# A hybrid decoder step on one core: cross-half scores one step later, and three sets of 128x128 tiles turned by VectorE in 32x32 blocks instead of by TensorE

## The chip, the cores and the metric

One core of one Trainium2 chip runs the whole step. The metric is the device time in microseconds (us) of the launch, as the median of several runs. The engines are named as the profile names them: PE (TensorE, matmuls; PEld its weight loads), DVE (VectorE), ACT (ScalarE), POOL (GpSimd), SP (SyncE). Engines run their own instruction queues and wait for each other by semaphores; a DMA is issued by an instruction in one engine's queue and lands later.

## The reference, cut to what matters

One decoder layer, 256 prompt tokens and 8 sample tokens (264 columns), model width 2048:

```python
z = h @ w_in                                   # 2048 -> one wide projection for three mixers
y_a = spatial_gating(u, layernorm(v), w_s, b_s)    # A: s = (w_s * lower triangle) @ v per 128-token chunk and group, 8 groups
o_hg, S_hg = gated_linear_recurrence(q, k, v, log_f, s0)   # B: HGRN2, 8 heads
o_g, S_g = gated_linear_recurrence(...)                     # C: GLA, 4 heads
merged = sum over n of gates[n] * (branches[n] @ w_branch[n])
x = x + gt1 * rmsnorm(merged @ w_out)
y2 = square(relu(h2 @ w_mlp_up)) @ w_mlp_down   # 2048 -> 8192 -> 2048
x = x + gt2 * rmsnorm(y2)                       # wanted with tokens in rows
```

Recurrence per head and token: `S = diag(f) S + k v^T`, `o = S^T q`, with `f` from `log_f`. `w_s` has the shape 8 x 128 x 128. Outputs are the two y, the recurrences' last states, and the normalised v rows.

## The kernel before, in words

**Layout and the weight stream.** Activations stand channels in partitions, tokens along the row ("turned", 264 columns). Each product with a weight matrix is done as three fp32r matmuls per 128x128 weight tile (whi with xh, whi with xl, wlo with xh). A *granule* is 512 KB of weights, 4 k-tiles by 2 output tiles, so 24 matmuls of 128x264 into one PSUM tile `mm` (`granule`, L713). `Stream` (L635) loads the raw weights on SP's queue into 4 buffers, casts them to `whi` on ACT (L673) and subtracts to get `wlo` on DVE (L677), two 128x512 halves per granule, into 6 split buffers; the splits run two granules ahead of the matmuls.

**What sets the order.** The program is written out granule by granule. After each granule `background()` (L785) advances a step counter `now`, runs what stands in the list `later`, and pumps three queues of generators: `bt` for turned rows, `bg` for the mixers, `bs` for the samples' recurrences. A generator that yields `READY` is not resumed before the next step. `slot()` (L747) places collected small products (the mixers' 32x32 level products, the samples' products, the ada products) between granules. In the first part, up to the projection, every engine keeps the program's order; in the mixers PE and POOL do, and in the last phase (the MLP) only PE, the other engines' order being set by the tile scheduler.

**Turning by `Rows`.** `Rows` (L837) turns blocks of channels x tokens: two DVE stream transposes (L850) that turn each 32x32 square in place, a DMA of 512 KB to DRAM scratch `rows_d` (L853), and one step or more later four DMAs of 128 KB back (L859), which put the squares where they belong. Both kinds of DMA are issued by POOL. `gone()` does the transposes and the DMA out; the rows come back by way of `bt`.

**Mixer A** (`mixer_a`, L948). `wsT`, the eight turned tiles of `w_s` times the triangle `triu`, is made by eight PE transposes in two groups of four (an identity as the weights, `cst`, into a PSUM tile `sm`) and two DVE multiplications out of PSUM (L139). `w_s` is the third of four constants that come by `const_a` at granules 8, 10, 12 and 14 of the last chunk but one, after `cst` and the masks at granule 7.

**Mixers B and C** (`mixer_r`, L1322), called for two HGRN2 groups of four heads (groups 0 and 1) and one GLA group (group 2). Within 32 tokens the scores come from level products, between 32-token blocks and 64-token blocks from cross products; last the cross-half scores: `kd` and `qd` (128 tokens to 128 tokens) are made by a subtraction, two exponentials (ACT, L1414) and two DVE multiplications (L139), `kd` is also turned by a `Rows`, and then four products of `kd` and `qd`, L1428, go to `sm` and are copied to `attx` (ACT, L1430). The output products follow, `outputs()` (L1488) turns them and copies the rows (L1497), `finish` (L1504) adds the samples' columns (PE transposes, copies L1513), and `parts_b` (L1580) multiplies by the gate (L1584) and splits the result for the branch's product with `w_branch`.

**The last down-projection** (`down`, L1857, f = NFB-1). For each output pair m = 0..6 (two granules each): the sum comes out of PSUM (L142), `gated` (L1626) scales it to `g` (128 x 2 x 264), and one step later four PE transposes (L96, `to_tokens`) put `g` with tokens in rows into PSUM, from where ACT (L1660) and DVE (L1661) copy 128x256 each into `yt`. The tail (m = 7, row sums, the last norm, the sum with x and the stores) uses `yt`.

Of the kernel before, what the change touches and what calls it, by code (L numbers as in the profile page):

```python
# [7 lines left out]
F32 = mybir.dt.float32  # L8
# [7 lines left out]
P = 128  # L16
# [19 lines left out]
CHUNKS = (2, 2, 4, 4, 4)  # L36
# [36 lines left out]
def hybrid_step_kernel(  # L73
# [55 lines left out]
    def sm(shape=None):  # L129
        return psm.tile(shape or [P, 512], F32, tag="sm", name=nm("sm"))  # L130
# [700 lines left out]
        return linear(win, 0, KT, c0, width, hH, hL)  # L831


    rows_d = dp.tile([13, P, 1024], F32, tag="rows_d", name="rows_d")
    n_turned = [0]

    class Rows:  # L837
# [67 lines left out]
    def const_a(src):  # L905
        consts_a.append(blk([P, 8, P]))
        nc.sync.dma_start(consts_a[-1], src)

    srcs_a = [
        sgu_ln_g[0].partition_broadcast(P).rearrange("p (g n) -> p g n", g=8),  # L910
        sgu_ln_b[0].partition_broadcast(P).rearrange("p (g n) -> p g n", g=8),
        sgu_w_s[0].rearrange("g n m -> n g m"),
        sgu_b_s[0].rearrange("g n -> (g n)").partition_broadcast(P).rearrange("p (g n) -> p g n", g=8),
    ]
    def to_tokens(vt):
# [30 lines left out]


    def mixer_a():  # L948
        lng, lnb, wsr, bsb = consts_a
        lng, lnb = (v.rearrange("p g n -> p (g n)") for v in (lng, lnb))  # L950
        vr, vtk = rows_a.rows, []
        wsT = blk([P, 8, P])
        w00 = tmp([P, 8], "w00", 1)
        for gg in range(2):
            ps = sm()
            for i in range(4):
                T.transpose(ps[:, i * P:(i + 1) * P], wsr[:, 4 * gg + i, :], ident)
            yield
            mul(wsT[:, 4 * gg:4 * gg + 4, :], ps.rearrange("p (g n) -> p g n", g=4), triu.unsqueeze(1).to_broadcast([P, 4, P]))
        yield  # L960
        vs = tmp([P, 8, NS], "vsa", 1)
        w8 = tmp([P, 8, NS], "vsb", 1)
        r8 = tmp([P, NS], "vsr", 1)
# [139 lines left out]
    for ci, n in enumerate(CHUNKS):  # L1103
        final = ci == len(CHUNKS) - 1
        gn = 4 // n
        ng = len(begin) // gn
        if not final:
            nxt = parts[ci].paced()
        for gi in range(ng):
            if ci or gi:  # L1110
                accs = [new_acc() for _ in range(gn)]
            todo = begin[gi * gn:gi * gn + gn]

            def evict(acc):

                c0, dst, fn = todo.pop(0)
                z = acc[:, :, 0:NT]
                if ci:
                    add(dst, dst, z)
                elif todo:  # L1120
                    S.copy(dst, z)
                else:
                    V.tensor_copy(dst, z)
                if final and fn is not None:
                    after.append((dst, fn))

            def between():

                step[0] += 1
                if not final:  # L1130
                    next(nxt, None)

            load_due()
            if ci or gi:
                granule(win, 0, n, begin[gi * gn][0], gn * CW, accs, hH, hL, k0, True, True, evict, between)
            else:
                first_granule(accs, evict, between)
            if ci == 0 and gi < 2:
                x_transposed(4 + 2 * gi, early[gi])
            if ci == 0 and 1 <= gi < 5:  # L1140
                x_transposed(2 * gi + 6)
            while after:
                dst, fn = after.pop(0)
                S.activation(dst, dst, fn)
            if final:
                if gi in (6, 12, 18):
                    rounds.steps()
                if gi in (0, 2, 6, 8, 12, 14, 18):
                    rounds.load()
                if gi in (6, 7, 8, 9):  # L1150
                    rows_a.half((gi - 6) // 2, gi % 2)
                if gi in (8, 10):
                    rows_a.out(gi // 2 - 4)
                if gi in (11, 13):
                    rows_a.back((gi - 11) // 2)
                now[0] += 1
                if gi >= 12:
                    bg.pump(1.0)
            if ci == len(CHUNKS) - 2 and 7 <= gi < 16:
                if gi == 7:  # L1160
                    nc.sync.dma_start(cst[:, 256:904], consts[:, 256:904])
                    nc.sync.dma_start(msk, masks.rearrange("p (l t) -> p l t", l=6))
                elif gi % 2 == 0:
                    const_a(srcs_a.pop(0))
        if not final:
            run(nxt)
        k0 += n
# [154 lines left out]
    def mixer_r(G):  # L1322
# [99 lines left out]
        kd_rows = Rows([kd])  # L1422
        yield from kd_rows.gone()
        yield READY
        attx = blk([P, 4, P])
        ps = sm([P, 4, P])
        for h in range(4):
# [235 lines left out]
    def block_rows(m, g):  # L1663
# [5 lines left out]
        for t in range(2):  # L1669
            squares(m, t, g, pt)  # L1670

    def norms(meanwhile):

        ps = sm([P, 2 + NS])
# [182 lines left out]
    def down(f, ah, al):  # L1857
        for m in range(8):
# [7 lines left out]
                add(dst, dst, z)  # L1866
            if f == NFB - 1:
                g = gated(m, dst, G2)
                later.append((now[0], lambda m=m, g=g: put_rows(m, to_tokens(g), yt)))

    zs = begin_up()
    order.__exit__(None, None, None)
# [3 lines left out]
    for f in range(NFB):  # L1876
        nxt = up(f + 1) if f + 1 < NFB else None
        if f == NFB - 1:
            rounds.drain()
            mul(G2, mod[:, 5 * KT:6 * KT, :], gpost2T.unsqueeze(2).to_broadcast([P, KT, NC]))  # L1880
            yt = [[blk([P, 1024]) for _ in range(2)] for _ in range(2)]
        last = pend
        down(f, *pend)
        pend = nxt
# [150 lines left out]
```

## Time and profile before

| what | value |
|---|---|
| median of 3 runs | 1780.88 us (1779.7 to 1781.59) |
| profiled execution | 1784.03 us, span 1782.2 us |
| PE busy | 1759.0 us (99%), 16866 matmuls |
| DVE busy | 1191.7 us (67%), 2094 instructions |
| ACT busy | 998.4 us (56%) |
| POOL busy | 175.6 us (10%), 293 instructions |
| bytes moved by DMA | 455.67 MB, mean 256 GB/s |

The span is the profiled execution from its first to its last instruction; the profiled execution's own time is 1.83 us longer, and 3.15 us longer than the median of the runs. Rows of the timeline give the start, the time from the first start to the last end, the engine, the line, the operation, and how many were joined (x4); in brackets stands the idle time before and what ended it. Matmuls overlap in a pipeline: one of 0.28 us follows the other at 0.11 us.

### The profile page before, as it was taken

The numbers are of one execution on the slowest core, as the hardware profiler recorded it, in microseconds if no ns is written. First come the engines' busy times: TensorE is split into PE (matmuls) and PEld (weight loads), VectorE is DVE, ScalarE is ACT, GpSimd is POOL, SyncE is SP. The second block draws the span as 40 slices with busy tenths as digits, with TensorE's granted clock in tenths as the row PEclk, the third lists the DMA queues.
The fourth block names the chain that finished last, engine by engine and source line by source line (L and its number), as shares of the span: only waits on it lengthen the run. The fifth ranks groups of instructions, "written<-read, shape, count | busy, mean of one in ns | idle before, by whom it ended". The sixth has DMA issues, their size and how long they took to land.

```text
span 1782.2 us, 42021 instructions
## 1 busy us (share of the span) xinstructions
PE 1759.0 (99%) x16866; PEld 1677.1 (94%) x16866; DVE 1191.7 (67%) x2094; ACT 998.4 (56%) x1810; POOL 175.6 (10%) x293
## 2 busy tenths in 40 slices
PE   7999999999999999999999999999999999999998
PEld 5899999999998989999999989999999999999997
DVE  5666669887786886656556666545666666666666
ACT  5444456766766666445445666555454545454554
POOL 4222010122121123200000010000000000000000
PEclk9999999999999999999999999999999999999999
DMA  9998799899999899988876847786666666666663
GB/s 352 399 346 301 240 315 302 261 327 314 323 289 298 289 327 297 374 241 271 272 249 215 306 128 239 234 265 189 197 194 196 196 197 194 198 194 197 194 195 114
DMA packets 334547, 455.67 MB, mean 256 GB/s; under 512 B 15986, under 2 KB 277984, under 8 KB 334352
## 3 DMA queue, kind: packets, MB, share of 16 engines
q1 hardware_dynamic: 312160, 381.05, 66.1%
q0 software_dynamic: 21552, 71.48, 11.6%
q8 instruction: 132, 2.16, 0.5%
q14 instruction: 63, 0.52, 0.1%
q10 hardware_dynamic: 640, 0.47, 0.1%
HBM read 434.42 MB, written 18.51 MB: 254 GB/s over the span
## 4 chain that ended last, share of the span: by engine, by line
PE 94%; DMA 2%; DVE 1%; issue 1%; ACT 1%; POOL 0%; SPq 0%; ACTq 0%; DVEq 0%; POOLq 0%
PE mm L92 85%; PE ada L92 5%; PE sm L92 3%; PE sm L96 1%; DMA raw<-in_w_in_dram 1%; DMA vbc<-vs_d 1%; DMA b<-in_x_prompt_dram 0%; DVE wlo L677 0%; DMA b<-in_w_ada_dram 0%; DVE b L142 0%; DVE b L1775 0%; DMA out_dram<-st 0%; DVE st L1306 0%; ACT b L148 0%; DVE b L145 0%
## 5 line engine op out<-in xcount | busy, mean ns | idle before, releaser
L92 PE MATMUL mm<-b,whi 128*128 128x264 f32 x9248 | 1579.0, 277 | 1.9 <-ACT gt L1549 0.9
L92 PEld LDWEIGHTS mm<-b,whi 128*128 128x128 f32 x9248 | 1395.2, 189 | 35.8 <-issue 18.2
L92 PE MATMUL mm<-b,wlo 128*128 128x264 f32 x4624 | 1276.1, 276 | 0.4 <-DVE wlo L677 0.4
L677 DVE TENSOR_TENSOR wlo<-raw,whi 128x512 fp32r<-128x512 f32 x1118 | 758.5, 689 | 427.2 <-ACT whi L673 423.3
L673 ACT CAST whi<-raw 128x512 fp32r<-128x512 f32 x1118 | 680.8, 617 | 632.0 <-DVE wlo L677 325.8
L92 PEld LDWEIGHTS mm<-b,wlo 128*128 128x128 f32 x4624 | 873.9, 189 | 0.9 <-DVE wlo L677 0.8
L142 DVE TENSOR_TENSOR b<-b,mm 128x528 f32<-128x528 f32 (+1 forms) x137 | 95.6, 699 | 72.2 <-PE mm L92 65.8
L1965 POOL TENSOR_TENSOR gs<-b,G 128x16 f32<-128x16 f32 x1 | 0.2, 221 | 714.0 <-DVE b L142 714.0
L92 PE MATMUL ada<-b,cT 128*32 128x256 f32 (+2 forms) x896 | 66.0, 425 | 1.6 <-DMA b<-in_w_ada_dram 1.4
L92 PEld LDWEIGHTS ada<-b,cT 128*32 128x32 f32 x896 | 26.6, 113 | 31.6 <-issue 17.9
L537 POOL DMA_DIRECT2D b<-in_w_ada_dram x64 | 46.3, 726 | 44.9 <-PE ada L92 35.3
L1307 POOL DMA_DIRECT2D out_dram<-st x32 | 23.5, 735 | 209.2 <-DVE st L1306 204.0
L673 ACT CAST whi<-araw 128x512 fp32r<-128x512 f32 x38 | 23.2, 619 | 27.7 <-PE mm L92 24.0
L1306 DVE SCALAR_TENSOR_TENSOR st<-vbc,b,st 128x128 f32<-128x128 f32 (+1 forms) x96 | 32.3, 390 | 6.0 <-ACT st L1304 3.2
L1304 ACT ACTIVATE st<-st,fs 128x128 f32<-128x128 f32 (+1 forms) x96 | 35.1, 427 | 1.9 <-DMA st<-in_state_gla_dram 1.9
L139 DVE TENSOR_TENSOR b<-b,b 128x512 f32<-128x512 f32 (+1 forms) x49 | 34.6, 720 | 2.0 <-ACT b L1414 0.5
L92 PE MATMUL ada<-araw,cT 128*32 128x512 f32 x256 | 34.6, 600 | 0.0
L859 POOL DMA_DIRECT2D b<-rows_d x52 | 28.6, 556 | 27.9 <-ACT whi L673 7.3
L677 DVE TENSOR_TENSOR wlo<-araw,whi 128x512 fp32r<-128x512 f32 x38 | 24.5, 685 | 1.3 <-ACT whi L673 1.3
L92 PE MATMUL sm<-b,b 128*32 128x32 f32 (+2 forms) x320 | 22.9, 237 | 2.4 <-DVE b L139 2.4
L145 DVE TENSOR_TENSOR b<-gt,b 128x528 fp32r<-128x528 f32 x32 | 22.7, 709 | 3.2
L145 DVE TENSOR_TENSOR b<-b 128x1024 f32<-128x1024 f32 (+1 forms) x24 | 24.5, 1021 | 0.1
(308 smaller groups left out, 826.5 us busy)
## 6 DMA issues: line engine op xcount, KB each, us to landing
raw<-in_w_in_dram SPq DMA_DIRECT2D x225, 512.0 KB, 5.7
raw<-in_w_mlp_down_dram SPq DMA_DIRECT2D x128, 512.0 KB, 3.6
raw<-in_w_mlp_up_dram SPq DMA_DIRECT2D x125, 512.0 KB, 3.9
araw<-in_w_ada_dram SPq DMA_DIRECT2D x64, 512.0 KB, 6.2
b<-in_w_ada_dram SPq DMA_DIRECT2D x64, 512.0 KB, 6.5
b<-in_w_ada_dram POOLq DMA_DIRECT2D x48, 512.0 KB, 9.8
raw<-in_w_branch_dram SPq DMA_DIRECT2D x48, 512.0 KB, 5.5
raw<-in_w_out_dram SPq DMA_DIRECT2D x32, 512.0 KB, 4.6
```

The costliest lines, as they stand in the source:

```text
L92: return nc.tensor.matmul(out, w, x, **kw)
L96: return nc.tensor.transpose(*a)
L139: V.tensor_tensor(o, a, b, op=ALU.mult)
L142: V.tensor_tensor(o, a, b, op=ALU.add)
L145: V.tensor_tensor(o, a, b, op=ALU.subtract)
L537: queue.dma_start(w[:, i], w1[k * P:(k + 1) * P, :, self.k0 * P:(self.k0 + self.n) * P])
L673: self.last = [S.copy(hi, raw).ins, None]
L677: self.last[1] = V.tensor_tensor(lo, raw, hi.bitcast(F32), op=ALU.subtract).ins
L859: nc.gpsimd.dma_start(t[32 * q:32 * q + 32, :].rearrange("p (s c) -> p s c", s=4), rows_d[self.d0 + i].rearrange("(s p) (q c) -> q p s c", ...
L1304: S.activation(st[:, i, :], st[:, i, :], AF.Copy, scale=fs[:, h0 + i, b:b + 1])
L1306: V.scalar_tensor_tensor(st[:, i, :], v[:, i, :], k[:, h0 + i, NP + b:NP + b + 1], st[:, i, :], ALU.mult, ALU.add)
L1307: nc.gpsimd.dma_start(G.s_out(b, h0, nh), st)
```

## The change

Three parts.

1. `mixer_r`: one more `yield READY` before the cross-half scores, in each of the three groups.
2. `w_s` is loaded first of the four constants (granule 7, ahead of `cst`; the masks move to granule 8, the other three to 10, 12 and 14). It is turned by a `Rows`: two DVE transposes at granules 11 and 13, out at 14, back at 18. `mixer_a` multiplies the landed rows by the triangle; its eight PE transposes go, and it has one yield fewer.
3. The last down-projection, m = 0..3: a new class `Pairs` collects two `g` (eight DVE transposes of 128x256 in all, L1696, two for each m), sends each pair out as 512 KB, brings it back in four DMAs one step later, and two steps after that copies it into `yt` with one ACT and one DVE copy of 128x512 (L1713). The sixteen PE transposes of these four m and their eight copies out of PSUM go. m = 4..6 stay as they were.

In the changed kernel lines up to L955 stand where they were or one off; later lines are 10 or 11 lower down (L1306 is L1316, L1584 is L1595, L1661 is L1672). `rows_d` has 16 slots instead of 13.

```diff
 def mixer_a():
-        lng, lnb, wsr, bsb = consts_a
+        _, lng, lnb, bsb = consts_a
...
         for gg in range(2):
-            ps = sm()
-            for i in range(4):
-                T.transpose(ps[:, i * P:(i + 1) * P], wsr[:, 4 * gg + i, :], ident)
+            mul(
+                wsT[:, 4 * gg:4 * gg + 4, :].rearrange("p k (s f) -> p k s f", s=4),
+                rows_w.rows[0][:, gg],
+                triu.rearrange("p (s f) -> p s f", s=4).unsqueeze(1).to_broadcast([P, 4, 4, 32]),
+            )
             yield
-            mul(wsT[:, 4 * gg:4 * gg + 4, :], ps.rearrange("p (g n) -> p g n", g=4), triu.unsqueeze(1).to_broadcast([P, 4, P]))
-        yield
...
             if ci == len(CHUNKS) - 2 and 7 <= gi < 16:
                 if gi == 7:
+                    const_a(srcs_a.pop(0))
+                    rows_w = Rows(consts_a[0:1], lambda b, r: b[:, 4 * r:4 * r + 4, :].rearrange("p k (q f) -> p k q f", q=4))
                     nc.sync.dma_start(cst[:, 256:904], consts[:, 256:904])
+                elif gi == 8:
                     nc.sync.dma_start(msk, masks.rearrange("p (l t) -> p l t", l=6))
-                elif gi % 2 == 0:
+                elif gi < 15 and gi % 2 == 0:
                     const_a(srcs_a.pop(0))
+            if ci == len(CHUNKS) - 2:
+                if gi in (11, 13):
+                    rows_w.half(0, (gi - 11) // 2)
+                if gi == 14:
+                    rows_w.out(0)
+                if gi == 18:
+                    rows_w.back(0)
...
 def mixer_r(G):
         kd_rows = Rows([kd])
         yield from kd_rows.gone()
+        yield READY
         yield READY
...
+    class Pairs:
+        def __init__(self, rows, landed, then):
+            self.rows, self.landed, self.then = rows, landed, then
+        def put(self, m, g):
+            i = m % 2
+            if i == 0:
+                self.r = Rows([None])
+                self.r.ts[0] = blk([P, 1024])
+            to = self.r.ts[0].rearrange("p (q r k f) -> p r k q f", q=4, r=2, k=4)
+            for t in range(2):
+                V.transpose(to[:, t, 2 * i:2 * i + 2], g[:, :, t * P:(t + 1) * P].rearrange("p k (q f) -> p k q f", q=4))
+            if i:
+                self.r.out(0)
+                self.soon(1, self.back, m // 2, self.r)
+        def soon(self, n, f, *a):
+            later.append((now[0] + n, lambda: f(*a)))
+            later.sort(key=lambda x: x[0])
+        def back(self, b, r):
+            r.back(0)
+            self.soon(self.landed, self.natural, b, r.rows.pop())
+        def natural(self, b, v):
+            w = slice(b % 2 * 512, b % 2 * 512 + 512)
+            for t in range(2):
+                (V.tensor_copy if t else S.copy)(self.rows[t][b // 2][:, w].rearrange("p (k s f) -> p k s f", k=4, s=4), v[:, t])
+            self.then(b, w)
...
 down, f == NFB - 1:
-                later.append((now[0], lambda m=m, g=g: put_rows(m, to_tokens(g), yt)))
+                later.append((now[0], lambda m=m, g=g: put_rows(m, to_tokens(g), yt) if m > 3 else pairs.put(m, g)))
...
+            pairs = Pairs(yt, 2, lambda b, w: None)
```

**What stands where, first place: the cross-half scores of group 1.** In these rows `b<-b,b` on DVE is an operand being made (`b_7930` is `qd`, `b_7929` is `kd`), `wlo` the splits of coming granules, `sm<-b,b 128x128 x4` on PE the four scores, `sm<-b,att` the output products behind them. PE before:

```order
L92 MATMUL mm_8050<-b_5668,wlo_7917 128x264
L92 MATMUL sm_8086<-b_7930,b_7929 128x128 x4
L92 MATMUL sm_8096<-b_4791,att 128x128 x4
L92 MATMUL mm_8050<-b_5672,whi_7963 128x264
L92 MATMUL mm_8050<-b_5673,whi_7963 128x264
L92 MATMUL mm_8050<-b_5672,wlo_7964 128x264
```

DVE before:

```order
L677 TENSOR_TENSOR wlo_7964<-raw_7818,whi_7963 128x512
L139 TENSOR_TENSOR b_7929<-b_7929,b_6628 128x1024
L677 TENSOR_TENSOR wlo_7968<-raw_7818,whi_7967 128x512
L1306 SCALAR_TENSOR_TENSOR st_7724<-vbc_7877,b_6628,st_7724 128x128 x4
L677 TENSOR_TENSOR wlo_8011<-raw_7873,whi_8010 128x512
L677 TENSOR_TENSOR wlo_8015<-raw_7873,whi_8014 128x512
L1306 SCALAR_TENSOR_TENSOR st_7875<-vbc_7937,b_6628,st_7875 128x128 x4
L142 TENSOR_TENSOR os_1207_7208<-os_1207_7208,sm_8030 128x128
L139 TENSOR_TENSOR b_7930<-b_7930,b_176 128x512
L850 STREAM_TRANSPOSE b_7974<-b_7929 128x4x4x32 x2
```

PE now, where `b_8117` is `qd` and `b_8116` is `kd`:

```order
L92 MATMUL mm_8127<-b_2727,wlo_8157 128x264
L92 MATMUL sm_8284<-b_8117,b_8116 128x128 x4
L92 MATMUL sm_8294<-b_4790,att 128x128 x4
L92 MATMUL mm_8324<-b_334,whi_8190 128x264
L92 MATMUL mm_8324<-b_335,whi_8190 128x264
L92 MATMUL mm_8324<-b_334,wlo_8191 128x264
```

DVE now:

```order
L139 TENSOR_TENSOR b_8117<-b_8117,b_176 128x512
L139 TENSOR_TENSOR b_8116<-b_8116,b_6666 128x1024
L677 TENSOR_TENSOR wlo_8100<-raw_7959,whi_8099 128x512
L677 TENSOR_TENSOR wlo_8104<-raw_7959,whi_8103 128x512
L1567 SCALAR_TENSOR_TENSOR b_7834<-gt_8038,mm_8040 128x528
L850 STREAM_TRANSPOSE b_8163<-b_8116 128x4x4x32 x2
L677 TENSOR_TENSOR wlo_8153<-raw_8005,whi_8152 128x512
L677 TENSOR_TENSOR wlo_8157<-raw_8005,whi_8156 128x512
L677 TENSOR_TENSOR wlo_8191<-raw_8073,whi_8190 128x512
```

Before, the product that makes `qd` stands on DVE behind `wlo_8011` and `wlo_8015`, which belong to the granule after the one (`whi_7963`) that PE begins right behind the scores. Now it stands ahead of `wlo_8153` and `wlo_8157`, which belong to the granule that PE ends right ahead of the scores.

**Second place: the output rows of group 1 and the start of branch 1.** On DVE, `L1497` (now `L1508`) is the copy of the landed rows, `L1513` (`L1524`) are the copies of `finish`, `L1584` (`L1595`) the gate of `parts_b`, `b<-cst,b` and the products with `cst` the start of group 2. DVE before, two pieces of one stretch:

```order
L677 TENSOR_TENSOR wlo_8525<-raw_8396,whi_8524 128x512
L1497 COPY b_8612<-b_8530 128x4x128
L1346 SCALAR_TENSOR_TENSOR b_3947<-cst,b_3947 128x264
L139 TENSOR_TENSOR b_8655<-b_3946,cst 128x1024
L1573 SCALAR_TENSOR_TENSOR b_8155<-b_8155,mm_8363 128x528
L677 TENSOR_TENSOR wlo_8564<-raw_8443,whi_8563 128x512
```

```order
L677 TENSOR_TENSOR wlo_8888<-raw_8733,whi_8887 128x512
L1513 COPY b_6750<-sm_8903 128x4x8
L1513 COPY b_8612<-sm_8907 128x4x8
L1584 SCALAR_TENSOR_TENSOR b_6750<-b_6750,vec,b_8155 128x1056
L677 TENSOR_TENSOR wlo_8892<-raw_8733,whi_8891 128x512
```

DVE now:

```order
L677 TENSOR_TENSOR wlo_8786<-raw_8674,whi_8785 128x512
L1508 COPY b_8791<-b_8716 128x4x128
L139 TENSOR_TENSOR b_8834<-b_3951,cst 128x1024
L677 TENSOR_TENSOR wlo_8819<-raw_8714,whi_8818 128x512
L1524 COPY b_6741<-sm_8840 128x4x8
L1524 COPY b_8791<-sm_8844 128x4x8
L677 TENSOR_TENSOR wlo_8823<-raw_8714,whi_8822 128x512
L1584 SCALAR_TENSOR_TENSOR b_8126<-b_8126,mm_8681 128x528
L1595 SCALAR_TENSOR_TENSOR b_6741<-b_6741,vec,b_8125 128x1056
```

Between the copy of the rows and the copies of `finish` stood 30 rows of DVE; now there are two.

**Third place: the last down-projection.** On PE, `sm<-cst,gt` are the four transposes of one m. PE before, between two granules:

```order
L92 MATMUL mm_23798<-b_22720,whi_23709 128x264
L92 MATMUL mm_23798<-b_22719,wlo_23710 128x264
L96 MATMUL sm_23833<-cst,gt_23792 128x128 x4
L92 MATMUL mm_23798<-b_23007,whi_23746 128x264
L92 MATMUL mm_23798<-b_23008,whi_23746 128x264
```

PE now, at the same two granules:

```order
L92 MATMUL mm_23804<-b_22726,whi_23715 128x264
L92 MATMUL mm_23804<-b_22725,wlo_23716 128x264
L92 MATMUL mm_23804<-b_23013,whi_23752 128x264
L92 MATMUL mm_23804<-b_23014,whi_23752 128x264
L92 MATMUL mm_23804<-b_23013,wlo_23753 128x264
```

DVE before, from one `g` to the next:

```order
L1635 TENSOR_SCALAR gt_23961<-b_15026,G_15024 128x256
L142 TENSOR_TENSOR a_2227_13612<-a_2227_13612,vt_23960 128x264
L139 TENSOR_TENSOR gs_13613<-b_15026,G_15024 128x16
L142 TENSOR_TENSOR a_2227_13612<-a_2227_13612,vt_23960 128x264
L677 TENSOR_TENSOR wlo_23994<-raw_23872,whi_23993 128x512
L677 TENSOR_TENSOR wlo_23998<-raw_23872,whi_23997 128x512
L1661 COPY b_23719<-sm_24003 128x256
L677 TENSOR_TENSOR wlo_24035<-raw_23916,whi_24034 128x512
L142 TENSOR_TENSOR b_15026<-b_15026,mm_23968 128x528
```

DVE now, where the first landed pair (`b_24001`) is copied:

```order
L1646 TENSOR_SCALAR gt_24045<-b_15032,G_15030 128x256
L142 TENSOR_TENSOR a_2232_13618<-a_2232_13618,vt_24044 128x264
L139 TENSOR_TENSOR gs_13619<-b_15032,G_15030 128x16
L1696 STREAM_TRANSPOSE b_24006<-gt_24045 128x2x4x32
L142 TENSOR_TENSOR a_2232_13618<-a_2232_13618,vt_24044 128x264
L677 TENSOR_TENSOR wlo_24078<-raw_23955,whi_24077 128x512
L1696 STREAM_TRANSPOSE b_24006<-gt_24045 128x2x4x32
L677 TENSOR_TENSOR wlo_24082<-raw_23955,whi_24081 128x512
L1713 COPY b_23725<-b_24001 128x512
L677 TENSOR_TENSOR wlo_24112<-raw_23999,whi_24111 128x512
```

PE goes from granule to granule without the transposes, DVE has two transposes for each m in place of one copy out of PSUM, and the copy of a landed pair stands ahead of `wlo_24112`.

More of the change, by code (lines that the diff above doesn't have):

```diff
@@ L831, in zin @@
         return linear(win, 0, KT, c0, width, hH, hL)
-    rows_d = dp.tile([13, P, 1024], F32, tag="rows_d", name="rows_d")
+    rows_d = dp.tile([16, P, 1024], F32, tag="rows_d", name="rows_d")
     n_turned = [0]
@@ L909, in hybrid_step_kernel @@
     srcs_a = [
+        sgu_w_s[0].rearrange("g n m -> n g m"),
         sgu_ln_g[0].partition_broadcast(P).rearrange("p (g n) -> p g n", g=8),
         sgu_ln_b[0].partition_broadcast(P).rearrange("p (g n) -> p g n", g=8),
-        sgu_w_s[0].rearrange("g n m -> n g m"),
         sgu_b_s[0].rearrange("g n -> (g n)").partition_broadcast(P).rearrange("p (g n) -> p g n", g=8),
```

## The prediction

> **What bounds the kernel now.** I read the page's busy shares first, then busy time by stage, PE's waits, and the timeline round the one long wait.
>
> ```profile
> span 1782.2 us, 42021 instructions
> PE 1759.0 (99%) x16866; PEld 1677.1 (94%) x16866; DVE 1191.7 (67%) x2094; ACT 998.4 (56%) x1810; POOL 175.6 (10%) x293
> PE 94%; DMA 2%; DVE 1%; issue 1%; ACT 1%; POOL 0%; SPq 0%; ACTq 0%; DVEq 0%; POOLq 0%
> ```
>
> PE is busy for 1759.0 of 1782.2 us and carries 94% of the chain that ended last. A term therefore counts only if it is PE work, a PE wait, or a lower granted clock. By stage (span, then busy time of PE, PEld, DVE, ACT and POOL, granted clock, DMA share, GB/s):
>
> ```profile
> 260.00:300.00 40.00, 40.00 (x355) 38.35 (x352) 34.56 (x90) 20.01 (x33) 4.03 (x7) 1.00 0.98 327
> 300.00:540.00 240.00, 240.00 (x2863) 224.45 (x2862) 193.43 (x363) 171.78 (x342) 50.69 (x82) 1.00 0.94 300
> 540.00:760.00 220.00, 216.33 (x2228) 199.61 (x2228) 158.58 (x307) 139.68 (x292) 49.40 (x79) 0.99 0.95 316
> 1730.00:1766.00 36.00, 35.87 (x320) 35.67 (x319) 27.76 (x60) 21.00 (x42) 0.00 (x0) 1.00 0.39 118
> ```
>
> The spatial weights are turned in the first row, the scores belong to the next two, the last down-projection to the last. PE has no gap in the first two; 3.67 us are missing in the third. PE's waits that fall there; one is long:
>
> ```profile
> PE sm L92 <- DVE b L139: 2.4, 1, 2.4
> ...
> PE mm L92 <- ACT gt L1549: 0.9, 1, 0.9
> ```
>
> ```profile
> 549.26 0.63 ACT L1414 ACTIVATE b<-b 128x512 f32<-128x512 f32 x1
> 549.92 0.69 DVE L139 TENSOR_TENSOR b<-b,b 128x512 f32<-128x512 f32 x1 [0.50 <-ACT b L1414]
> 550.53 1.30 DVE L850 STREAM_TRANSPOSE b<-b 128x512 f32<-128x512 f32 x2
> 550.76 1.13 PE L92 MATMUL sm<-b,b 128*128 128x128 f32 x8 [2.37 <-DVE b L139]
> ```
>
> ```profile
> 551.00:552.00 1.00, 1.00 (x10) 1.00 (x10) 1.00 (x3) 0.07 (x1) 0.00 (x0) 0.91 1.09 381
> 552.00:553.00 1.00, 1.00 (x7) 1.00 (x6) 1.00 (x2) 0.51 (x1) 0.88 (x2) 0.50 1.01 407
> 553.00:554.00 1.00, 1.00 (x7) 1.00 (x6) 0.00 (x1) 0.42 (x1) 0.43 (x1) 0.50 1.00 406
> 554.00:555.00 1.00, 1.00 (x6) 1.00 (x6) 0.00 (x0) 0.94 (x5) 0.00 (x0) 0.50 0.99 294
> 555.00:556.00 1.00, 1.00 (x10) 1.00 (x9) 0.00 (x0) 0.33 (x2) 0.00 (x0) 0.88 0.99 319
> ```
>
> These are the cross-half scores of group 1. ACT's exponential ends at 549.89, DVE's product (qd) at 550.6, and PE stood idle 2.37 us for it. Right behind the gap the granted clock falls: 0.91, 0.50 three times, 0.88. What is missing from full speed adds up to 0.09 + 1.50 + 0.12 = 1.71 us. The stall cost 2.37 + 1.71 = 4.08 us.
>
> **Part 1, the extra step: −4.08 us.** By the order of the changed program a whole granule of PE work stands between the place of the scores before and now. A granule lasts 24 matmuls, half of the 5.40 us that 48 take (rows below), 2.70 us. PE, free at 548.4, would have other work until 551.1; qd is done at 550.6. DVE also no longer has two splits of a later granule ahead of qd. So the wait goes, with 0.5 us to spare, and with it the low clock. Bounds: 0 if the operand comes as much later as PE does, −4.08 if all goes; I take all, because the group's other operand chain is unchanged in length. Groups 0 and 2 have no such wait, so the step gives nothing there. What is late next is ACT's copy to `attx` and the output products, which have a level of slack: their only reader is the same generator, one step later too. The queues passed are POOL's (kd's DMA out and back, still put out before the scores) and DVE's.
>
> [...]
>
> The whole mixer part is dealt out anew by the step and by what part 2 takes from PE: the places where PE leaves the granules' stream number 109 in the old order and 112 in the new, and six of the old ones go, so nine are new. Each such place costs PE a restart, priced next.
>
> **Parts 2 and 3, PE's transposes: −0.88 and −1.76 us.** The chain's rows in the last down-projection (start, us), and PE's timeline at the spatial weights:
>
> ```profile
> 1731.47 5.40 PE mm L92 x48
> 1736.87 0.44 PE sm L96 x4
> 1737.31 5.40 PE mm L92 x48
> ```
>
> ```profile
> 263.24 0.60 PE L96 MATMUL sm<-cst,b 128*128 128x128 f32 x4
> 263.60 0.47 PE L92 MATMUL mm<-b,whi 128*128 128x264 f32 x2
> ```
>
> Four transposes lengthen the period from 5.40 to 5.84 us: 0.44 us. At the spatial weights four of the same shape take 0.36 us from their start to that of the next granule, so the other 0.08 is the restart of the stream. Last down: 4 x 0.44 = 1.76 us. Spatial weights: 2 x 0.44 = 0.88 us. The nine new restarts give back 9 x 0.08 = 0.7 us (0 if they hide, twice that if weight loads start cold too; I take the row's value).
>
> What replaces them is off PE, if covered. First DVE and the landings:
>
> ```profile
> L850 DVE STREAM_TRANSPOSE b<-b 128x512 f32<-128x512 f32 x26 | 17.8, 699 | 1.3 <-ACT b L1469 1.3
> L1661 DVE COPY b<-sm 128x256 f32<-128x256 f32 x14 | 5.8, 418 | 0.6 <-ACT b L1660 0.6
> 1736.00:1742.00 6.00, 6.00 (x56) 6.00 (x55) 4.89 (x13) 3.84 (x8) 0.00 (x0) 1.00 0.58 175
> ```
>
> ```profile
> rows_d<-b POOLq DMA_DIRECT2D x13, 512.0 KB, 6.0
> b<-rows_d POOLq DMA_DIRECT2D x52, 128.0 KB, 7.0
> DMA to landing us min/median/max: 2.8/6.9/8.5
> 253.70 2.21 POOL L859 DMA_DIRECT2D b<-rows_d  x4
> raw<-in_w_in_dram SPq DMA_DIRECT2D x225, 512.0 KB, 5.7
> raw<-in_w_mlp_down_dram SPq DMA_DIRECT2D x128, 512.0 KB, 3.6
> ```
>
> In the last down-projection DVE works 4.89 of 6.00 us, 4.76 of one 5.84 us period. Per m it loses a copy (0.42) and gains two half-size transposes (2 x 0.35): 5.04 of the new 5.40. Where a pair's copy (0.42, the same 512 elements) also falls, 5.46: over by 0.06, once or twice, behind splits that stand two granules (5.4 us) ahead. Nothing, while that lead lasts. POOL is idle there.
>
> The landing: DMA out 6.0, three further issues of 0.55 (a quarter of 2.21), back 7.0: 14.7 us; at the shortest 2.8 + 1.65 + 2.8 = 7.3, at the longest 8.5 + 1.65 + 8.5 = 18.7. By the new order the copies stand five granules (13.5 us) and four (10.8) behind the DMA out. The medians come from the mixers, with DMA shares near 0.95; here the share is 0.58, and raw loads land in 3.6 us where they took 5.7. In that ratio 14.7 becomes 9.3, inside both. I take 0; the far end is rival B.
>
> [...]
>
> For the spatial weights, DVE gets two transposes (1.40 us) and the triangle product reads SBUF instead of PSUM; 1 MB more of DMA.
>
> ```profile
> b<-in_sgu_w_s_dram SPq DMA_DIRECT2D x1, 512.0 KB, 6.7
> 196.00:202.00 6.00, 6.00 (x56) 6.00 (x55) 4.78 (x10) 4.53 (x9) 1.53 (x4) 1.00 0.41 126
> ```
>
> Its load lands 6.7 us after issue and is first used four granules (10.8 us) later; DVE has 1.2 of 6 us free. From the DMA back (granule 18) to `mixer_a` are tens of us. Swapping constants on SP's queue puts one 512 KB load ahead of two raw loads, into a stretch where the DMA share is 0.41 and PE waits for nothing. Nothing.
>
> **A cost of the shift.** Group 1's output rows are now copied right at the start of branch 1, not five granules ahead of it.
>
> ```profile
> 589.84 0.43 DVE L1497 COPY b<-b 128x512 f32<-128x512 f32 x1 [2.14 <-DMA b<-rows_d]
> 600.00:610.00 10.00, 9.84 (x144) 8.14 (x143) 10.00 (x16) 6.66 (x13) 0.00 (x0) 1.00 0.63 182
> 609.69 0.38 PE L96 MATMUL sm<-cst,os 128*128 128x128 f32 x2
> 615.41 1.30 PE L92 MATMUL sm<-b 128*32 128x32 f32 x128
> 617.63 1.25 DVE L145 TENSOR_TENSOR b<-b,b 128x1056 fp32r<-128x1056 f32 x1
> ```
>
> Before, DVE waited 2.14 us for that landing, and PE was short 0.16 us ten us later, where DVE was full. The same wait now has the gate products and the branch's splits close behind it. Those had slack: from `finish` on PE (609.69) it is four granules (10.8) and the level products (1.3) to the branch's first granule, 621.8 us, and DVE's last split (L145) ended at 618.9, some 3 us before. Bounds: 0, and 2.14 us in full; nearer the row, in which PE felt 0.16: +0.2.
>
> **Sum:** −4.08 − 0.88 − 1.76 + 0.7 + 0.2 = −5.82 us on the span of 1782.2. The profiled execution took 1784.03, the median of the runs 1780.88; I take the same difference from the median: 1775.1 us.
>
> **Rivals.** A measurement tells 0.2%, 3.56 us, from no change: faster is below 1777.3, slower above 1784.4.
>
> A, the stall stays or comes back elsewhere. The mixers' order is new everywhere, and another operand may be short as this one was. For it: one wait in three groups was long with the old order, with nothing in it to forbid one in the new. Against it: PE waited for nothing else longer than 0.9 us in 460 us of such work. It gives −5.82 + 4.08 = −1.74: 1779.1, no change.
>
> B, the pairs land late. At the longest 18.7 us the second copy is 7.9 us late on DVE; two granules' lead less the fuller DVE, about 4, leaves 3.9 us of idle PE, and 1.71 of low clock as above: +5.6. It gives 1780.7, no change. Against it, the ratio of landings.
>
> C, slower: group 1's rows land so late that branch 1 waits. Place: DVE's copy now L1508, with the gate products and splits queued behind it. To lose 5.82 and 3.56 more, PE must lose 9.4: 7.7 us idle and 1.71 of clock, so with 3 us of slack the copy must wait 10.7 us. One raw load in that stretch did take 13.88 us:
>
> ```profile
> 717.76 13.88 DMA raw<-in_w_in_dram
> ```
>
> If both ways took that, 29.4 instead of 14.7, the copy would wait 2.14 + 14.7 = 16.8: 13.8 idle, 1.71 of clock, 1780.88 − 5.82 + 15.5 = 1790.6. No row of `rows_d` took over 8.5, so it is unlikely.
>
> **How the numbers follow.** Forecast 0.71, A 0.17, B 0.06, C 0.05, and 0.01 for a saving of under 3.56 by small costs. Faster 0.71, no change 0.24, slower 0.05. The forecast's own range: down by 0.7 (free restarts), 1.2 (the lowest run against the median) and 0.9 (PE's second wait above, should it go): 1772.3; up to 1777.3. The 8-in-10 range must reach past A: 1772 to 1779.6 leaves out C, most of B, a little of A and of the low end.
>
> **What would show it.** Right: no PE wait on L139 at L92 `sm`; granted clock 1.00 in 545–760; a period of 5.40 us in the last down-projection for m = 0..3 with no L96 between; 24 fewer L96 transposes; copies L1713 with no wait on `rows_d`; DVE's 128x256 transposes near 350 ns. Wrong: a new PE wait of 2 us or more followed by clock 0.50; DVE waiting at L1508 with `wlo` late behind it; PE idle near 1750.

## The result and the profile after

The changed kernel takes 1779.28 us (median of 22 runs, 1776.47 to 1782.55), the kernel before 1781.55 us (22 runs, 1778.48 to 1784.21). The ratio is 0.9986 with an interval of 0.998 to 0.9993: 2.5 us faster (1.2 to 3.6), where 5.8 us were forecast. The time lies in the range given, near its upper end; by size it is the case "no change" of the prediction, not its likeliest, and it lies outside the forecast's own range of 1772.3 to 1777.3.

The first profile of after shows much more than that. The page:

```profile
span 1774.6 us, 42035 instructions
PE 1755.4 (99%) x16842; PEld 1672.7 (94%) x16842; DVE 1195.1 (67%) x2104; ACT 997.3 (56%) x1808; POOL 184.3 (10%) x308
PE 97%; DMA 1%; DVE 1%; ACT 0%; SPq 0%; issue 0%; DVEq 0%
```

The span is 7.6 us shorter than that of before, three times the difference of the medians. The reason is the pair of executions: the profile of before ran 1784.03 us, among its slowest, and that of after 1776.47, the fastest of its 22. Two profiles alone would have told a wrong size here: 1.7 us of the 7.6 are the fall of the clock in the profile of before. What they tell is where each part went. The stage of the mixers in after (PE's busy time was 216.33 in the same stretch of before):

```profile
540.00:760.00 220.00, 219.81 (x2277) 203.81 (x2276) 164.27 (x303) 144.21 (x299) 49.69 (x79) 1.00 0.93 302
```

The row "PE sm L92 <- DVE b L139: 2.4" is gone from PE's waits, and the granted clock is 1.00. Gone too is the row "PE mm L92 <- ACT gt L1549: 0.9". The two operands of group 1 on DVE, and the scores on PE:

```profile
549.62 1.83 DVE L139 TENSOR_TENSOR b<-b,b 128x512 f32<-128x512 f32 x2
```

```profile
563.60 1.05 PE L92 MATMUL sm<-b,b 128*128 128x128 f32 x8
```

The chain through the last down-projection:

```profile
1725.00 24.52 PE mm L92 x218
1749.52 0.44 PE sm L96 x4
1749.96 5.40 PE mm L92 x48
```

The first row runs through m = 0..3 with no L96 in it; the four transposes return with m = 4, 0.44 us as before. What took their place, the group of DVE's transposes and the first copy of a landed pair:

```profile
L1696 DVE STREAM_TRANSPOSE b<-gt 128x256 f32<-128x256 f32 x8 | 3.4, 434 | 0.0
```

```profile
1744.00 0.43 DVE L1713 COPY b<-b 128x512 f32<-128x512 f32 x1 [1.04 <-DMA b<-rows_d]
```

DVE waited 1.04 us for the landing, and PE for nothing. The DMA share between the DMA out and the copy is another than the prediction took from before. First before, at the same granules, then after (the share stands second from the end):

```profile
1738.00:1750.00 12.00, 12.00 (x109) 12.00 (x109) 9.79 (x22) 7.36 (x14) 0.00 (x0) 1.00 0.60 185
```

```profile
1732.00:1744.00 12.00, 12.00 (x109) 12.00 (x109) 9.95 (x24) 6.78 (x13) 3.26 (x6) 1.00 0.93 270
```

So both effects that the prediction named are there. Where the rest of the forecast gain went is the question of the experiments.

For them each trace is cut at the same places: every 24th matmul into a PSUM tile `mm`, counted from the first one of all, which is near a granule's first. Three stretches matter: granules 40 to 84 (the load, the turning and the old transposes of the spatial weights, about 159 to 293 us), 84 to 240 (mixers and branches), 560 to 577 (last down-projection). "Step", "weights" and "pairs" are the three parts of the change.

| kernel profiled | 40–84, us | 84–240, us | 560–577, us |
|---|---|---|---|
| before | 134.44 | 518.59 | 49.24 |
| before, second profile | 134.69 | 517.97 | 49.24 |
| pairs | 134.44 | 516.74 | 47.58 |
| step | 134.44 | 514.38 | 49.24 |
| step, pairs | 134.44 | 512.66 | 49.66 |
| all (after) | 134.59 | 513.43 | 47.58 |
| all, second profile | 137.07 | 512.97 | 47.58 |
| all, old deal of the mixers | 135.04 | 512.79 | 47.58 |
| all, pairs copied a step earlier | 136.65 | 513.32 | 48.21 |
| all, weights late | 135.51 | 513.04 | 47.58 |
| all, weights late, pairs copied a step later | 136.81 | 513.50 | 48.80 |
| weights, pairs | 134.26 | 520.80 | 47.58 |
| weights | 135.31 | 520.30 | 49.24 |
| weights, old deal of the mixers | 134.51 | 517.51 | 49.24 |

The rows "weights, pairs" and "weights" have another deal of the mixers, which moves 1.7 us of products across the cut at granule 240: granules 240 to 560 took 903.0 and 903.1 us there, and 904.7 to 904.8 in all the others.

### The profile page after: what moved, and what is told of

The parts are those of the page before. It is cut to its first block, busy times and chain, and to the rows that moved or that the text cites. A ratio compares the mean times of both kernels' runs of the same rounds, so it can differ in the third digit from the quotient of the medians.

```text
span 1774.6 us, 42035 instructions
## 1 busy us (share of the span) xinstructions
PE 1755.4 (99%) x16842; PEld 1672.7 (94%) x16842; DVE 1195.1 (67%) x2104; ACT 997.3 (56%) x1808; POOL 184.3 (10%) x308
## 4 chain that ended last, share of the span: by engine, by line
PE 97%; DMA 1%; DVE 1%; ACT 0%; SPq 0%; issue 0%; DVEq 0%
PE mm L92 88%; PE ada L92 5%; PE sm L92 4%; PE sm L96 1%; DMA b<-in_w_ada_dram 1%; DMA b<-in_x_prompt_dram 0%; DVE b L1819 0%; DVE wlo L677 0%; DVE b L142 0%; ACT b L148 0%; DVE b L145 0%; SPq L537 0%; SPq L189 0%; DVE vt L1851 0%; ACT vt L1853 0%
## 5 line engine op out<-in xcount | busy, mean ns | idle before, releaser
L92 PE MATMUL mm<-b,whi 128*128 128x264 f32 x9248 | 1577.4, 277 | 1.2 <-DVE b L142 0.5
L92 PEld LDWEIGHTS mm<-b,whi 128*128 128x128 f32 x9248 | 1394.3, 189 | 36.0 <-issue 19.2
L92 PE MATMUL mm<-b,wlo 128*128 128x264 f32 x4624 | 1275.4, 276 | 0.0
L92 PEld LDWEIGHTS mm<-b,wlo 128*128 128x128 f32 x4624 | 873.5, 189 | 0.1
L853 POOL DMA_DIRECT2D rows_d<-b x16 | 9.0, 564 | 768.8 <-DVE b L1696 685.5
L92 PE MATMUL ada<-b,cT 128*32 128x256 f32 (+2 forms) x896 | 66.7, 423 | 1.5 <-DMA b<-in_w_ada_dram 1.4
L92 PEld LDWEIGHTS ada<-b,cT 128*32 128x32 f32 x896 | 26.4, 112 | 32.3 <-issue 17.3
L859 POOL DMA_DIRECT2D b<-rows_d x64 | 35.2, 556 | 48.9 <-PE mm L92 18.4
L1316 DVE SCALAR_TENSOR_TENSOR st<-vbc,b,st 128x128 f32<-128x128 f32 (+1 forms) x96 | 32.4, 390 | 5.3 <-DMA vbc<-vs_d 3.7
L139 DVE TENSOR_TENSOR b<-b,b 128x512 f32<-128x512 f32 (+1 forms) x49 | 34.3, 719 | 0.9 <-ACT b L1404 0.4
L92 PE MATMUL ada<-araw,cT 128*32 128x512 f32 x256 | 34.7, 600 | 0.0
L1893 ACT ACTIVATE b<-vt 128x528 fp32r<-128x528 f32 x32 | 22.9, 717 | 1.0
```

Of the source, the lines that this page charges most:

```text
L92: return nc.tensor.matmul(out, w, x, **kw)
L139: V.tensor_tensor(o, a, b, op=ALU.mult)
L859: nc.gpsimd.dma_start(t[32 * q:32 * q + 32, :].rearrange("p (s c) -> p s c", s=4), rows_d[self.d0 + i].rearrange("(s p) (q c) -> q p s c", ...
L1316: V.scalar_tensor_tensor(st[:, i, :], v[:, i, :], k[:, h0 + i, NP + b:NP + b + 1], st[:, i, :], ALU.mult, ALU.add)
L1893: S.activation(apart(a), by_two(rl), AF.Square)
```

## The experiments

Ratios are to the kernel before on the same chip, with 95% intervals; one thousandth is 1.8 us. My theory after the result was that the 4.08 us stall had been an accident of the one profiled execution (theory L): its row of ACT showed a cast that had waited 3.05 us for a raw load. The rival was that it is real and something else gives time back.

**The step alone.**

```diff
         yield from kd_rows.gone()
+        yield READY
         yield READY
```

> Only the extra step before the cross-half scores. Theory L (lottery): the 4.08 us stall of group 1 came from a raw load that landed late in the one profiled execution and is missing from most executions of the kernel before, so the step is worth nothing: ratio 1.000, within 1 us. Theory R (real, given back): the stall is in every execution, the step takes it out, and something else of the change gives 3 us back: about 4 us faster, ratio 0.9977.

Measured: 0.9986 (0.9978 to 0.9995), 2.4 us faster. Neither 0 nor, by its middle, 4.

**All but the step.**

```diff
         yield from kd_rows.gone()
-        yield READY
         yield READY
```

(against the changed kernel)

> The whole change without the extra step. Theory L: all of the gain is in the transposes taken from PE, 1.76 + 0.88 = 2.6 us: ratio 0.9985. Theory R: the stall stays, and what gives time back stays as well: no faster than the kernel before, 0 to 1 us slower.

Measured: 1.0007 (0.9998 to 1.0016), 1.3 us slower: theory L's 2.6 us gain is excluded.

**The weights alone** (the diff's parts on `srcs_a`, `mixer_a` and the last chunk but one).

> Only the spatial weights turned by VectorE. Both theories: 8 transposes fewer on PE, 0.9 us faster, ratio 0.9995, near what five rounds can tell. If the moved loads or the new order of the mixers cost something, it is slower here.

Measured: 1.0024 (1.0015 to 1.0033), 4.3 us *slower*, against 0.9 faster in both theories. PE's waits of this kernel:

```profile
PE sm L92 <- DVE st L1316: 2.0, 1, 2.0
```

and of "all but the step", which holds the same deal of the mixers, the timeline:

```profile
749.18 0.88 DVE L1316 SCALAR_TENSOR_TENSOR st<-vbc,b,st 128x256 f32<-128x256 f32 x2 [2.24 <-DMA vbc<-vs_d]
749.72 1.00 PE L92 MATMUL sm<-st,b 128*32 128x256 f32 x3 [2.95 <-DVE st L1316]
```

The eight transposes that go change the count by which small products are placed, and the mixers are dealt out anew. The wait at 550 us is gone in that deal without any extra step, and another stands at 749 us: a sample's state waits on DVE for a DMA, and PE for the state. A wait took the place of the one removed, by a part that was not meant to touch either. Where all of the 4.3 us went is not shown: the profile of this kernel is of the fastest of its eleven runs (1784.16 us), and its span is that of before within 0.2 us.

**The pairs alone** (class `Pairs`, its call and its instance).

> Only the four tiles of the last down-projection turned in pairs. Theory L: 1.76 us faster, ratio 0.9990, and the period of two granules 5.40 us in the profile. Theory R with the loss in the last down-projection: the copies of the landed rows hold VectorE, PE waits there for splits, and it is 0 to 3 us slower.

Measured: 0.9991 (0.9982 to 1.0), 1.6 us faster, and 47.58 against 49.24 us in the stretch 560–577: 1.66. This part is as forecast. Its mixers are those of before, so its profile shows the stall a second time:

```profile
546.19 1.14 ACT L673 CAST whi<-raw 128x512 fp32r<-128x512 f32 x2 [3.46 <-DMA raw<-in_w_in_dram]
550.72 1.13 PE L92 MATMUL sm<-b,b 128*128 128x128 f32 x8 [2.38 <-DVE b L139]
```

```profile
550.00:551.00 1.00, 0.28 (x2) 0.31 (x3) 1.00 (x2) 0.88 (x2) 0.00 (x0) 1.00 1.03 310
551.00:552.00 1.00, 1.00 (x11) 1.00 (x10) 1.00 (x3) 0.11 (x1) 0.00 (x0) 1.00 1.09 422
552.00:553.00 1.00, 1.00 (x11) 1.00 (x10) 0.96 (x2) 0.69 (x2) 0.91 (x2) 1.00 1.01 410
```

The same 2.38 us of idle PE, at the same place, behind the same late raw load; so theory L falls. But the granted clock (third column from the end) stays at 1.00. The stall belongs to the program, the fall of the clock behind it does not always come.

**The changed kernel again**, with three variants on one chip.

> The changed kernel once more, on the chip of the three variants beside it and with a second profile. Measured so far: ratio 0.9986, 2.5 us. Theory S (its first profile was its fastest execution, the usual one has a wait that this one lacked): 0.9986 again, and a profile some 2 us longer that names the wait. Theory C (the first comparison was low by chance): 4 to 5 us faster, 0.9975.

Measured: 0.9991 (0.9982 to 0.9999); theory S. Its second profile ran 2.6 us longer and names the places. Granules 40 to 84 took 137.07 us instead of 134.59:

```profile
225.74 1.66 ACT L673 CAST whi<-raw 128x512 fp32r<-128x512 f32 x3 [3.62 <-DMA raw<-in_w_in_dram]
```

```profile
227.85 0.46 PE L92 MATMUL mm<-b,whi 128*128 128x264 f32 x2 [1.54 <-DVE b L142]
```

ACT waited 3.62 us for a raw load, some 10 us after the DMAs back of the spatial weights (issued from 215.25 us on), and PE 1.54 us; that these DMAs made it late is not shown. PE's eight ada products at 277 us, whose weights were there in before, now wait in the first profile of after as well. Before, then after, first its matmuls and then its weight loads:

```profile
278.38 1.04 PE L92 MATMUL ada<-b,cT 128*32 128x512 f32 x8
```

```profile
276.91 1.85 PE L92 MATMUL ada<-b,cT 128*32 128x512 f32 x8
```

```profile
277.71 0.14 PEld L92 LDWEIGHTS ada<-b,cT 128*32 128x32 f32 x4 [0.68 <-DMA b<-in_w_ada_dram]
```

PE gets there 1.5 us earlier (0.9 by the transposes, the rest by an earlier start of the program), and the ada weights have not landed: the eight products take 1.85 us instead of 1.04. The 0.88 us saved on PE turned into a wait for a DMA 14 us later: granules 64 to 84 take 61.84 us in before and 61.82 in after. The DMA share from 260 to 300 us was 0.98 in before and 0.96 in after.

**Step and pairs, without the weights.**

> The change without its part on the spatial weights (the extra step and the pairs). Theory W (turning the spatial weights by VectorE costs time with the extra step too, as it did alone): the sum of the two parts alone, 2.4 + 1.6 = 4 us faster, ratio 0.9977, so faster than the whole change by 1.5 us. Theory N (it costs nothing here; the single parts were measured too high): 0.9 us slower than the whole change, 0.9991.

Measured: 0.9988 (0.9979 to 0.9996), 2.1 us: not told apart from the whole change. So the weights' part is worth nothing measurable beside the step; nor do the pairs add to the step's 2.4 us in these medians, though the stretch shows their 1.66 us wherever they landed in time. Its profile shows rival B of the prediction at work, in the last down-projection:

```profile
1746.73 0.62 ACT L1703 COPY b<-b 128x512 f32<-128x512 f32 x1 [5.40 <-DMA b<-rows_d]
1746.79 0.43 DVE L1703 COPY b<-b 128x512 f32<-128x512 f32 x1 [4.42 <-DMA b<-rows_d]
...
1750.34 0.66 PE L96 MATMUL sm<-cst,gt 128*128 128x128 f32 x4 [1.50 <-ACT gt L1639]
```

The first pair landed late, its copy held ACT, ACT's next `gt` came late, and PE waited 1.50 us: 49.66 us in 560–577, more than before the change. In the six other profiles whose copies stand alike (after, after again, pairs alone, all but the step, all with the old deal, all with the weights late) DVE waited 1.0 to 1.1 us and ACT 1.9 to 2.1 for that pair, and PE nothing: the stretch took 47.58.

**The weights alone, with the mixers dealt out as before.**

```diff
             mul(wsT ..., rows_w.rows[0][:, gg], triu ...)
+            T.n += 8
             yield
+        yield
```

> Only the spatial weights turned by VectorE, but with the mixers' products dealt out as in the kernel before: the count of PE instructions by which small products are placed goes on by the 16 that the eight transposes were, and the yield that the change drops is kept. Alone, the part was 4.3 us slower (1.0024). Theory D (the new deal of the mixers did that, by the wait at 749 us): 0.9 us faster, 0.9995. Theory L (the loads moved ahead, two more VectorE transposes or 1 MB more of DMA did it): still 4 us slower.

Measured: 1.0014 (1.0005 to 1.0022), 2.5 us slower; between the two theories of this run, and nearer its L. With the old deal the loss is 1.8 us less than without by the middles, but the two intervals overlap, so that the deal is part of the 4.3 us is likely and not shown. The profile has the stall at 550 us again (1.94 us), a wait of 1.8 us for ACT's `gt` at 735 us (0.6 to 1.4 in the profiles with before's mixers), 134.51 us in 40–84, and a slow start of the program (granules 0 to 20 took 76.87 us against 75.04 in before, where both programs are the same). No one row carries the 2.5 us; it stays open.

**All, with the mixers dealt out as for the step alone** (the changed kernel with the same two lines).

> The whole change with the mixers dealt out as in the kernel that has the extra step alone (same count, same yields). If the parts add up where the deal is unchanged: 2.4 + 1.6 + 0.9 = 4.9 us faster, 0.9972. If the moved loads or the turned rows of the weights cost time by themselves: as the whole change, 0.9986.

Measured: 0.9984 (0.9975 to 0.9992), 2.9 us faster. The best number of all, but the intervals overlap with the whole change's; the parts do not add up to 4.9.

**The landed pairs copied a step earlier.**

```diff
-            pairs = Pairs(yt, 2, lambda b, w: None)
+            pairs = Pairs(yt, 1, lambda b, w: None)
```

> The whole change with the landed pairs copied one step after the DMA back instead of two, so 2.7 us earlier in the program. In the profiles so far VectorE waited 0 to 4.4 us for the first pair. Theory B (the landing is at the edge of what the splits' lead hides): the wait grows to between 3 and 7 us, PE waits 1 to 3 us near 1745 us in the profile, and the kernel is 1 to 3 us slower than the whole change: ratio 0.999 to 1.000. Theory H (hidden with room to spare): as the whole change, 0.9988, no PE wait there.

Measured: 0.9986 (0.9978 to 0.9995), as the whole change. It does not decide between B and H, since the edit did not reach what it was for: DVE's and ACT's order is the scheduler's in this phase, and the copy of the first pair stands at the same place (DVE waited 0.8 us for it); only the order of PE's last transposes and their copies moved. The stretch 560–577 took 48.21 us, with 0.5 us of PE's waiting for ACT's `gt`.

**The weights turned late, constants loaded in the old order.**

```diff
+            if final:
...
+                if gi in (0, 2):
+                    rows_w.half(0, gi // 2)
+                if gi == 3:
+                    rows_w.out(0)
+                if gi == 6:
+                    rows_w.back(0)
```

> The whole change with the constants loaded in the order of the kernel before and the spatial weights turned only in the last chunk (transposes at its granules 0 and 2, out at 3, back at 6). Theory M (the moved 512 KB load and the two turning DMAs make raw loads late near 227 us, which PE felt in two of five profiles): no PE wait there, about 1 us faster than the whole change, 0.998. Theory N (those waits come by chance from other traffic): as the whole change, 0.9988, waits may show there or elsewhere.

Measured: 0.9993 (0.9984 to 1.0002), 1.2 us faster: theory M's 0.998 is excluded, and there is no gain over the whole change. Granules 40 to 64 took 72.60 us, as theory M says, but so they did in three of the seven profiles with the weights turned early; 64 to 84 took 62.91 instead of 61.82. It looks as if the same traffic moved its wait and did not remove it; one profile doesn't show it.

**The same, copied three steps after the DMA back.**

> As the kernel with the late spatial weights, and the landed pairs copied three steps after the DMA back. If both places lose time in the usual execution: 1 to 2 us faster than the whole change, 0.9975 to 0.998, no wait of VectorE for the pairs in the last down-projection. If not, as the whole change, or slower where the last copy now stands in the tail.

Measured: 1.0001 (0.9992 to 1.0011), no better than before: of the two cases named, the second, and its slower end. The first copy did not move here either; DVE waited 1.4 us for it, PE 1.1 us for ACT's `gt`, the stretch 560–577 took 48.80 us, and granules 64 to 84 took 64.21. That it is slower than the kernel above is not clear of noise.

**The kernel before, one more profile.**

> The kernel before, one more profile. Theory P (the 2.4 us wait for the operand belongs to the program, the fall of the clock behind it to chance): idle near 2.4 us at 550 us, and no stretch at 0.50 behind it more often than not. Theory A (both belong together): 2.4 us idle and 3.4 us at half clock.

Measured, timeline and windows:

```profile
550.92 1.41 PE L92 MATMUL sm<-b,b 128*128 128x128 f32 x5 [2.40 <-DVE b L139]
```

```profile
550.00:551.00 1.00, 0.08 (x1) 0.11 (x1) 0.92 (x2) 1.00 (x3) 0.00 (x0) 0.89 1.04 353
551.00:552.00 1.00, 1.00 (x5) 1.00 (x6) 1.00 (x3) 0.08 (x1) 0.00 (x0) 0.50 1.03 376
...
554.00:555.00 1.00, 1.00 (x10) 1.00 (x9) 0.00 (x0) 0.46 (x1) 0.00 (x0) 0.91 0.99 368
```

2.40 us idle once more, and this time the clock fell, as theory A has it. But with this stall there are now two profiles with a fall (before, twice), and two without (pairs alone, 2.38 us idle; weights with the old deal, 1.94 us): so A is excluded, theory P's first half holds, and its "more often than not" two in four cannot settle.

## Why the prediction was right or wrong

- **The step, −4.08 forecast, −2.4 (0.9 to 3.9) measured alone.** The mechanism was right: the scores start without a wait, in all eight profiles that hold the step. Mis-sized was the term "2.37 + 1.71": I took the clock's fall as part of the stall. It came in two of four profiles that hold the stall, so by my estimate (half of 1.71) it is worth some 0.9 us on the average. That explains half of the 1.7 us between forecast and measurement; the other half is inside the interval. The "0.5 us to spare" was far off too, on the safe side: in after DVE ends the operands at 551.45 us and the scores start at 563.60, so the scores moved by far more than one granule. A second wait went with the first, which the prediction had only at the low end of its range: PE's for ACT's `gt`, 0.9, 1.4 and 0.6 us in the three profiles with before's mixers and none in the eight with the step. It widens the gap to the 2.4 measured. What I also passed over is why the operand was late: a raw load that ACT got at 546.2 to 547.0 us in all four, behind which its exponential stood.
- **The pairs, −1.76 forecast, −1.6 (0 to 3.2) measured, −1.66 by the stretch.** Right, with the small price that 128x256 transposes took 434 ns, not half of 699. The cover was thinner than the working said. Scaled medians gave 9.3 us from the DMA out to the landing; in after it took 12.1 (out at 1731.88, copy at 1743.97), and DVE waited 1.04 us for the first pair. The step that failed there is the scaling by the DMA share of 0.58: that was before's, and with the pairs' own traffic the share is 0.93. The splits' lead hid the wait, except in the one profile where it was 4.4. Rival B, given 0.06, is a thing that happens in some executions (one of the seven profiles whose copies stand alike) rather than in all or none.
- **The weights, −0.88 forecast.** This is the term that failed. "Two groups of transposes at 0.44" is right as PE work: 0.88 us less. But I put the whole of it on the path because PE was busy without a gap. The seven profiles with the part as the change has it took 134.26 to 137.07 us for granules 40 to 84, 135.35 in the mean, where the five with the old transposes took 134.44 to 134.69, 134.49 in the mean: 0.9 us more, not 0.9 less, and the best of the seven is only 0.2 less. (With so wide a spread the mean says that nothing was gained rather than how much was lost.) The cover named was PE's lack of waits and a DMA share of 0.41; six microseconds further on that share is 0.74, and 0.98 from 260 us, and in after the ada weights that land there set the pace as soon as PE is early (the eight products took 1.85 us there instead of 1.04).
- **The new restarts, +0.7, and branch 1, +0.2.** No sign of the first as a cost: the stretch 84–240 fell from 516.7–518.6 (the three with before's mixers) to 512.7–514.4 (the eight with the step). For group 1's rows DVE waited 2.14 us in before and not at all in after, where PE has no wait between 600 and 640 us: 0.

```profile
602.49 0.42 DVE L1508 COPY b<-b 128x512 f32<-128x512 f32 x1
```

- **The sum.** With the measured terms, −2.4 − 1.6 + 0.9 = −3.1, against −2.5 measured (−1.2 to −3.6). That is an agreement inside wide intervals (each term is known to 1.5 us), not a proof. Against it: step and pairs together measured 2.1, not 4.0, and the mixers' stretch fell by some 4 us in the profiles (3.3 us from pairs alone, where the clock did not fall, to after), where the step alone measured 2.4. The profiles of before ran 1784.03 and 1783.4 us, both over 1.4 us above the medians of their comparisons; why, I could not settle.
- **The rivals.** A (the stall comes back elsewhere) did not happen in the change as it is, but it does in the very same change without the step, at 749 us. C did not happen. That the time lies in the range is in part luck: the range went past 1777.3 us only to take in A, and the time stands there for another reason.
- **The base.** The sum was taken from one execution and carried to the median by a constant difference, as if the median held all that the profile held, the fall of the clock included. With the 22 runs' median of before as the base the forecast would have been 1775.7 us instead of 1775.1.

## What to carry to other kernels

Before a stall's full length goes into a sum, part it: the idle time, which belongs to the order of the program and came back here in all four profiles that hold it (2.37, 2.40, 2.38 and 1.94 us), and what depends on chance behind it (the fall of the clock in two of these four, the late landing of a pair in one of seven), which is worth its share of executions. On an engine that is busy for 99%, look further: where the DMA share is near 1 (0.96 here from 260 to 300 us), work taken away can bring the engine earlier to the next landing and turn the gain into a wait there, as at the ada products (1.85 us instead of 1.04). A DMA share read before a change does not hold the traffic that the change adds (0.60 in before, 0.93 in after, between a pair's DMA out and its copy). And changing a count that places other work is a change of its own: price it by running that alone.

## What the runs showed of the hardware

The length of a gap in PE's work alone did not tell whether the granted clock would fall. It fell with gaps of 2.37 us (before), 2.40 us (before, second profile) and 2.95 us (all but the step). It stayed at 1.00 with gaps of 2.38 us (pairs alone), 2.00 us (weights), 1.94 us (weights, old deal) and 1.50 us (step and pairs). So 2.37 us with a fall and 2.38 us without one stand at the same four products; what decides is not shown. Each of the three falls lasted 3.4 us, worked out from the shares of its first and last microsecond, with 0.50 as the granted clock of the fall: in before from 551.82 to 555.24 (0.91 and 0.88), in its second profile from 550.78 to 554.18 (0.89 and 0.91), in "all but the step" from 750.18 to 753.60 (0.59 and 0.70):

```profile
749.00:750.00 1.00, 0.28 (x2) 0.14 (x2) 0.82 (x3) 0.00 (x0) 0.00 (x0) 1.00 1.08 274
750.00:751.00 1.00, 1.00 (x10) 0.44 (x12) 1.00 (x3) 0.00 (x0) 0.64 (x1) 0.59 1.17 304
751.00:752.00 1.00, 1.00 (x12) 0.39 (x8) 0.00 (x0) 0.00 (x0) 0.09 (x1) 0.50 0.96 351
752.00:753.00 1.00, 1.00 (x12) 0.21 (x2) 0.00 (x0) 0.00 (x0) 0.00 (x0) 0.50 1.10 392
753.00:754.00 1.00, 1.00 (x5) 0.00 (x0) 0.04 (x1) 0.69 (x2) 0.00 (x0) 0.70 1.11 411
```

The program's start varies as well: granules 0 to 20, the same instructions in all kernels, took 75.04 us in before, 75.07 in after and 76.87 in the weights with the old deal. PE's waits for ada weights add up to 1.4 us over the whole program in each of the first two and to 2.5 in the third; how much of the difference they make is not shown.
